# Four small edits to a hybrid decoder trunk: the lambda rows' tile and place, the step of the sums of squares, a PSUM bank passed over, the order of three ScalarE instructions

## The chip, the cores and the metric

The kernel runs on one core of one Trainium2 chip. The metric is the device time of one launch in microseconds (us), the median over runs; lower is better.

## What is computed

A decoder trunk of two layers over 512 tokens of width 1024, all in float32. Each sub-layer is normalised first (RMSNorm) and added back. Cut to what matters here:

```python
# layer 0: differential attention, 8 heads of 2 x 64, values 128 wide
qkv = rmsnorm(h, attn_norm) @ w_in
lam = exp(sum(lq1 * lk1)) - exp(sum(lq2 * lk2)) + lambda_init      # four rows of 64
logits = q @ k.T * 64**-0.5 + bias        # T5 relative bias, causal; two maps per head
p = softmax(logits);  attn = p[:, 0] - lam * p[:, 1]
h = h + (rmsnorm(attn @ v, subln) * (1 - lambda_init)) @ w_out
h = h + square(relu(rmsnorm(h) @ w1)) @ w2                        # MLP, 4096 wide
# layer 1: mLSTM, 4 heads, q and k 128 wide, v 256 wide
proj = rmsnorm(h, mlstm_norm) @ w_in      # q,k | v | output gate | i and f gates (8 columns)
q, k = silu(causal_conv(proj_qk, width=4))
num, den = gated causal sums over keys of (q.k) * v and of (q.k)
ht = num / max(|den|, exp(-m));  out = sigmoid(o_pre) * rmsnorm(ht) 
h = h + out @ w_out
h = h + square(relu(rmsnorm(h) @ w1)) @ w2
return rmsnorm(h, final_norm)
```

## The kernel before

Activations lie transposed, features on the 128 partitions and 512 tokens along the free axis: `h` is eight tiles of 128x512. Every operand of a large product is split in a high and a low part (`split`: ScalarE writes the high part with a Copy, VectorE the rest), and a product is three matmuls: high x high, high x low, low x high (`mm3`, lines 406 to 408; 438 to 440 for value products, 928 to 930 in the MLP's second half).

**Weights** come in units of 128x1024 through rings of three buffers `raw`, `whi`, `wlo` (`unit`, `issue`). SP loads `raw`; ScalarE and VectorE split it. For the query and key columns of the mLSTM it is done otherwise (lines 351 to 353): ScalarE writes `whi` and the negated high part into `wlo`, and GpSimd (POOL) issues a DMA that adds the weights onto `wlo`. The product of the unit waits for that transfer.

**Order.** TensorE's (PE) order is the program's. Each product step of three (or six) matmuls ends with `tick()`, which runs what was put off with `after(n, fn)`, n steps ahead. The order on the other engines is made by a scheduler from its own estimates; within an engine instructions run in order.

**Opening.** `arrive(k)` makes the operand of feature tile k (`operand`: `x_xh` on ScalarE, `x_xl` on VectorE, line 519). `square_in` adds up squares in `acc`, on POOL from k = 1. `attention` runs `group_mm` (32 steps: queries and keys of heads 0 and 1, four banks), then `values_of(0, "sc")` (16 steps: the values of heads 0 and 1, into two of the three "sc" banks), then per head two `ntile_mm` of 8 steps. At step `T_RS` `token_scale` splits `acc`, multiplies by ones (lines 541 and 542), and makes `rs`, the token scale, in `rsqrt2` (lines 555 to 559, three ScalarE and two VectorE steps in `chains`) and line 567. `head` evicts queries and keys times `rs` (lines 709, 710) and splits them into halves (716 to 720; the queries' low half on POOL, 719). `constants`, put off to step 31, loads the four lambda rows into a `tmp` tile (line 672), multiplies and sums them (673, 680) and writes `coef`. `bias_rows` makes the bias rows, which go to DRAM and come back skewed (lines 642 to 653), per head. The first score products (736, 737) use the same "sc" banks as the values: the second one waits for the last eviction of `values_of(0)` (`evict_v`, lines 587 and 588).

**mLSTM start.** Three banks are called "mm", three "ac", two "sc". `vpair_mm(x, 264)` makes the first values and the gate columns in one "mm" and three "ac" banks (`psv`), which `gates` evicts 12 steps later, behind `rs`. Then eight `ntile_mm` follow, queries and keys by turns, each evicted by `evict_qk`: times `rs` into the one `conv` tile (line 1054), three taps on VectorE (1058), a Sigmoid on ScalarE, a product (1063 or 1065), and a split whose low half is POOL's. `bank("mm")` takes the banks in turn, so the third `ntile_mm` comes to the "mm" bank that holds values. `gate_rows` (from 1095: transposes, scans 1097 and 1103, rows `gs`) and `gate_cols` (1115) run between the tiles at steps 28 and 62.

**mLSTM heads.** `squares` evicts the numerator (`of`), squares it, and reads the bank `pf` with an Exp into `dd` (line 1188); the head's next score product waits for that bank.

Of the kernel before, what the change touches and what calls it, by code (L numbers as in the profile page):

```python
# [19 lines left out]
P = 128  # L20
T = 512
D = 1024
KT = D // P
# [15 lines left out]

T_RS, T_RSC, T_CONST, T_BIAS, T_ROWS = 24, 39, 31, 4, 14
T_ONE, T_TWO = 3, 12


# [140 lines left out]
def trunk(ctx: ExitStack, tc, xT, wgt, wgt2, cols, rows, rel, consts, outT):  # L186
# [11 lines left out]
    def nm(s):  # L198
        return f"{s}_{next(names)}"
# [22 lines left out]
    def tmp(n=T):  # L222
        return sp.tile([P, T], F32, tag="tmp", name=nm("tmp"))
# [5 lines left out]
    def asf(t):  # L229
        return t.bitcast(F32)  # L230
# [19 lines left out]
    def act(out, x, func, **kw):  # L250
        name = {AF.Exp: LNSET, AF.Ln: LNSET, AF.Sigmoid: SGSET}.get(func)
        if name:
            tables(name)
        ins = nc.scalar.activation(out, x, func, **kw)  # L254
        if name:
            behind(ins, loaded["load"])
            loaded["uses"].append(ins)
# [7 lines left out]
    def after(n, fn):  # L265
        heapq.heappush(queue, (clock[0] + n, next(names), fn))
# [232 lines left out]
    def row_of(c, n):  # L499
        return bass.AP(tensor=rows.tensor, offset=rows.offset + c, ap=[[0, P], [1, n]])  # L500

    def col(c):
        return colt[:, c : c + 1]
# [8 lines left out]
    lneps = const_col(math.log(EPS), "lneps")  # L512


    def operand(k, g0, acc):
        hi = xp.tile([P, T], F32R, tag="x", name=nm("xh"))
        lo = xp.tile([P, T], F32R, tag="x", name=nm("xl"))
        act(hi, h[k], AF.Copy, scale=col(g0 + k))
        vec.scalar_tensor_tensor(lo, h[k], col(g0 + k), asf(hi), op0=ALU.mult, op1=ALU.subtract)  # L519
        if acc is not None:  # L520
            square_in(k, acc)
        return lambda: (hi, lo)
# [95 lines left out]
    def attention(x, acc):  # L618
        with ExitStack() as st:
# [47 lines left out]
            klow = [[ap_.tile([P, T], F32R, name=f"kl{b}{m}") for m in range(2)] for b in range(2)]  # L667
            STEPS = (((3, 0),), ((2, 0),), ((1, 0), (0, 256)))

            def constants():  # L670
                rowt, prod = tmp(), tmp()
                nc.gpsimd.dma_start(rowt[:, :256], row_of(0, 256))
                vec.tensor_tensor(
                    prod[:, 0:128].rearrange("p (a d) -> p a d", a=2),
                    rowt[:, 0:256].rearrange("p (a b d) -> p a b d", a=2, b=2)[:, :, 0],
                    rowt[:, 0:256].rearrange("p (a b d) -> p a b d", a=2, b=2)[:, :, 1],
                    op=ALU.mult,
                )
                dots = tmp()
                vec.tensor_reduce(  # L680
                    dots[:, 0:2], prod[:, 0:128].rearrange("p (a d) -> p a d", a=2),
                    axis=mybir.AxisListType.X, op=ALU.add,
                )
                act(dots[:, 0:2], dots[:, 0:2], AF.Exp)
                vec.memset(coef, 1.0)
                vec.tensor_tensor(dots[:, 2:3], dots[:, 1:2], dots[:, 0:1], op=ALU.subtract)
                for c in (1, 3):
                    vec.tensor_scalar(coef[:, c : c + 1], dots[:, 2:3], -LAM0, None, op0=ALU.add)
                vec.tensor_scalar(subw, col(C_SUB), -0.5 * (1.0 - LAM0), None, op0=ALU.mult)
                for pair in klow:  # L690
                    for m in range(2):
                        o = slice(64 - 64 * m, 128 - 64 * m)
                        vec.tensor_scalar(pair[m][o], ones_f[o].to_broadcast([64, T]), 0.0, None, op0=ALU.mult)
                filled(pth[:, 1408:1536], 0.0)
                filled(ptl[:, 1408:1536], 0.0)
# [119 lines left out]
            def values_of(j, tag="mm"):  # L815

                def done(ps, b):
                    until(lambda: summed[0] >= 2 * j)
                    if b == 0:
                        vt.clear()  # L820
                        new.append(value_tiles(vp))
                    evict_v(ps, b, rsc[0], *new[0])

                new = []
                vpair_mm(x, 256, done, tag)
                vt[j] = new[0]
# [4 lines left out]
            after(T_RSC, lambda: rsc.append(token_cols(rs)))  # L831
            ps = group_mm(x)
            head(0, ps[0], ps[1], T_ONE)
            head(1, ps[2], ps[3], T_ONE + T_TWO)
            values_of(0, "sc")
            for hd in range(2, AH):
                psq, psk = ntile_mm(x), ntile_mm(x)
                head(hd, psq, psk)
                if hd % 2 == 1 and hd < AH - 1:
                    values_of(hd // 2)  # L840
# [168 lines left out]
    def mlstm(x, acc):  # L1009
        with ExitStack() as st:  # L1010
# [60 lines left out]
            def gates(psv):  # L1071

                rsc.append(token_cols(rs))
                for tb in range(NB):
                    vec.scalar_tensor_tensor(gi[:, tb], psv[tb][:, 256:260], rsc[0][:, tb : tb + 1],
                                             gate_bias[:, 0:4], op0=ALU.mult, op1=ALU.add)
                    vec.scalar_tensor_tensor(gf[:, tb], psv[tb][:, 260:264], rsc[0][:, tb : tb + 1],
                                             gate_bias[:, 4:8], op0=ALU.mult, op1=ALU.add)
                vec.tensor_scalar(ab, gf, -1.0, None, op0=ALU.mult)
                vec.tensor_tensor(ab, ab, gf, op=ALU.min)  # L1080
                act(ab, ab, AF.Exp)
                act(ab, ab, AF.Ln, bias=1.0)
                vec.tensor_scalar(gf, gf, 0.0, None, op0=ALU.min)
                vec.tensor_tensor(gf, gf, ab, op=ALU.subtract)
                vt[0] = value_tiles(vp)
                for j in range(2):
                    evict_v(psv, j, rsc[0], *vt[0])
# [31 lines left out]
            def head(hd):  # L1119
# [56 lines left out]
                def squares():  # L1176
                    num0, num1, den = acc3
                    summed[0] += 1
                    pf = bank("sc")
                    mm(pf, sel[:, hs], gs[:, 1280:1792], start=True, stop=True)  # L1180
                    dd, d2, s0, s1 = scale_tile("rs2"), tmp(), chain("sq"), tmp()
                    of = [sg.tile([P, T], F32, tag="of", name=nm("of"), bufs=2) for _ in range(2)]
                    act(of[0], num0, AF.Copy)
                    vec.tensor_copy(of[1], num1)
                    act(s0, of[0], AF.Square)
                    act(s1, of[1], AF.Square)
                    pool.tensor_tensor(s0, s0, s1, op=ALU.add)
                    act(dd, pf, AF.Exp, scale=-2.0, bias=lneps)
                    act(d2, den, AF.Square, scale=math.sqrt(EPS))
                    vec.tensor_tensor(dd, dd, d2, op=ALU.max)  # L1190
                    after(D_MLS[hd][2], lambda: normed(s0, dd, of))
# [48 lines left out]

            after(T_MRS, lambda: token_scale(acc, rs))
            psv = vpair_mm(x, 264)
            after(T_GATES, lambda: gates(psv))
            after(T_GROWS, gate_rows)
            after(T_GCOLS, gate_cols)
# [174 lines left out]
```

## Time and profile before

| | |
|---|---|
| median of 3 runs | 1175.04 us (1174.48 to 1175.22) |
| the profiled execution | 1175.75 us, span 1174.0 us |
| mean granted clock of TensorE | 0.992 |
| TensorE busy | 1143.0 us, 97% |
| VectorE (DVE) busy | 899.4 us, 77% |
| ScalarE (ACT) busy | 616.4 us, 53% |
| GpSimd (POOL) busy | 191.7 us, 16% |
| read from HBM | 112.30 MB |

The profile is one execution. A timeline row gives start, length, engine, line of the kernel, operation, output tile<-inputs, shape and, in brackets, the idle time ahead of it and what ended that. A matmul's recorded length overlaps the next one's; what counts is the distance from start to start. An idle time costs something only on the engine that holds up the end, which is for the most part TensorE.

### The profile page before, as it was taken

How to read it: one execution, taken by the hardware profiler on the slowest of the kernel's cores; microseconds unless marked ns; L12 is line 12 of the kernel's file. 1: busy time of each engine (PE TensorE's matmuls, PEld its weight loads, DVE VectorE, ACT ScalarE, POOL GpSimd, SP SyncE). 2: the span in 40 equal slices, each digit the busy share in tenths (PEclk: the TensorE clock that was granted, in tenths of full speed). 3: DMA queues.
4: the chain of work that ended last, by engine and by line, in shares of the span. 5: the costliest groups of instructions: out<-in, count | busy, mean ns of one | idle time of the engine just before them, and what ended most of it. 6: DMA issues, size and time to landing. Idle time of an engine off the chain costs nothing.

```text
span 1174.0 us, 17210 instructions
## 1 busy us (share of the span) xinstructions
PE 1143.0 (97%) x6718; PEld 1006.1 (86%) x6718; DVE 899.4 (77%) x1371; ACT 616.4 (53%) x926; POOL 191.7 (16%) x186
## 2 busy tenths in 40 slices
PE   8899999999999999999999999999999999999996
PEld 5778888888898998998997789888889889889895
DVE  7789888587977866967968867766698687687786
ACT  6567777564534434434557547665454353353453
POOL 5432332040000000000132212233000000000001
PEclk9899999999999999999999999999999999999998
DMA  6622222143164264362366221123325525526412
GB/s 203 203 64 75 78 73 78 65 123 123 61 168 138 64 180 134 84 169 90 92 155 147 68 90 55 54 80 104 122 82 135 161 73 139 173 66 153 135 37 72
DMA packets 37745, 128.12 MB, mean 109 GB/s; under 512 B 4479, under 2 KB 6546, under 8 KB 37664
## 3 DMA queue, kind: packets, MB, share of 16 engines
q1 hardware_dynamic: 30288, 103.38, 27.6%
q0 software_dynamic: 6256, 22.07, 9.8%
q10 hardware_dynamic: 1120, 1.57, 0.4%
q8 instruction: 53, 0.87, 0.3%
q14 instruction: 28, 0.23, 0.1%
HBM read 112.30 MB, written 4.74 MB: 100 GB/s over the span
## 4 chain that ended last, share of the span: by engine, by line
PE 81%; DVE 11%; ACT 4%; DMA 2%; issue 2%; POOL 0%; DVEq 0%; SPq 0%; ACTq 0%; POOLq 0%
PE bank L407 15%; PE bank L408 15%; PE bank L406 15%; PE bank L929 8%; PE bank L930 8%; PE bank L928 8%; DVE tmp_tmp L1058 2%; PE bank L439 1%; PE bank L438 1%; PE bank L440 1%; DVE wlo L534 1%; DMA raw<-wgt 1%; ACT whi L254 1%; PE bank L736 1%; DVE kl L720 1%
## 5 line engine op out<-in xcount | busy, mean ns | idle before, releaser
L406 PE MATMUL bank<-x_xh,whi 128*128 128x512 f32 x640 | 254.1, 397 | 4.0 <-DVE vl_v L588 2.5
L407 PE MATMUL bank<-x_xl,whi 128*128 128x512 f32 x640 | 254.9, 398 | 0.6 <-DVE x_xl L519 0.6
L408 PE MATMUL bank<-x_xh,wlo 128*128 128x512 f32 x640 | 255.4, 399 | 0.0
L254 ACT ACTIVATE whi<-raw 128x1024 fp32r<-128x1024 f32 (+2 forms) x128 | 133.4, 1042 | 115.6 <-PE bank L929 43.3
L534 DVE TENSOR_TENSOR wlo<-raw,whi 128x1024 fp32r<-128x1024 f32 (+2 forms) x120 | 152.9, 1274 | 30.2 <-ACT whi L254 29.5
L929 PE MATMUL bank<-ul,whi 128*128 128x256 f32 x544 | 153.3, 282 | 0.1
L928 PE MATMUL bank<-uh,whi 128*128 128x256 f32 x544 | 153.3, 282 | 0.0
L930 PE MATMUL bank<-uh,wlo 128*128 128x256 f32 x544 | 153.2, 282 | 0.0
L406 PEld LDWEIGHTS bank<-x_xh,whi 128*128 128x128 f32 x640 | 122.8, 192 | 32.2 <-DVE vl_v L588 3.0
L407 PEld LDWEIGHTS bank<-x_xl,whi 128*128 128x128 f32 x640 | 121.4, 190 | 28.1 <-DVE x_xl L519 1.3
L408 PEld LDWEIGHTS bank<-x_xh,wlo 128*128 128x128 f32 x640 | 121.1, 189 | 27.1 <-DVE wlo L534 0.2
L949 POOL DMA_DIRECT2D h<-work x24 | 20.8, 865 | 511.6 <-DVE work L946 392.5
L929 PEld LDWEIGHTS bank<-ul,whi 128*128 128x128 f32 x544 | 102.7, 189 | 0.5 <-DVE ul L534 0.3
L928 PEld LDWEIGHTS bank<-uh,whi 128*128 128x128 f32 x544 | 103.0, 189 | 0.1
L930 PEld LDWEIGHTS bank<-uh,wlo 128*128 128x128 f32 x544 | 102.8, 189 | 0.0
L254 ACT ACTIVATE uh<-chains 128x1792 fp32r<-128x1792 f32 (+1 forms) x38 | 56.9, 1497 | 57.6 <-DVE chains L889 57.4
L534 DVE TENSOR_TENSOR ul<-chains,uh 128x1792 fp32r<-128x1792 f32 (+1 forms) x38 | 67.3, 1771 | 23.8 <-ACT uh L254 23.3
L882 DVE SCALAR_TENSOR_TENSOR tmp_tmp<-bank,rs_rs 128x512 f32<-128x512 f32 x64 | 44.0, 688 | 44.7 <-PE bank L408 44.5
L530 POOL TENSOR_TENSOR acc_acc<-acc_acc,tmp_tmp 128x512 f32<-128x512 f32 x31 | 50.9, 1642 | 157.5 <-ACT tmp_tmp L254 152.5
L254 ACT ACTIVATE whi<-wsums 128x1024 fp32r<-128x1024 f32 x46 | 48.7, 1059 | 48.2 <-PE bank L929 30.2
L439 PE MATMUL bank<-wlo,x_xh 128*128 128x256 f32 (+1 forms) x256 | 72.2, 282 | 1.7 <-DVE wlo L534 1.7
L438 PE MATMUL bank<-whi,x_xh 128*128 128x256 f32 (+1 forms) x256 | 72.6, 284 | 0.0
(332 smaller groups left out, 2683.2 us busy)
## 6 DMA issues: line engine op xcount, KB each, us to landing
raw<-wgt SPq DMA_DIRECT2D x156, 512.0 KB, 3.8
rawx<-wgt SPq DMA_DIRECT2D x32, 512.0 KB, 4.1
h<-work POOLq DMA_DIRECT2D x24, 512.0 KB, 5.8
wlo<-wgt POOLq DMA_DIRECT2D x8, 512.0 KB, 7.3
skew<-frd POOLq DMA_DIRECT2D x8, 320.0 KB, 6.8
bias_bias<-skew POOLq DMA_DIRECT2D x8, 256.0 KB, 3.1
outT<-h SPq DMA_DIRECT2D x6, 256.0 KB, 2.5
raw<-wgt SPq DMA_DIRECT2D x2, 528.0 KB, 3.6
```

What stands on the lines that cost most here:

```text
L254: ins = nc.scalar.activation(out, x, func, **kw)
L406: mm(ps, whi, x[0], start=first, stop=False)
L407: mm(ps, whi, x[1], start=False, stop=False)
L408: mm(ps, wlo, x[0], start=False, stop=last)
L438: mm(ps, xh, hi[:, c], start=k == 0, stop=False)
L439: mm(ps, xh, lo[:, c], start=False, stop=False)
L530: (eng or pool).tensor_tensor(acc, acc, s, op=ALU.add)
L534: (eng or vec).tensor_tensor(lo, src, asf(hi), op=ALU.subtract)
L882: vec.scalar_tensor_tensor(m, p, 0.0, rs, op0=ALU.max, op1=ALU.mult)
L928: mm(out[name], hi[:, n], uh[:, t], start=first, stop=False, skip_group_check=late)
L929: mm(out[name], hi[:, n], ul[:, t], start=False, stop=False, skip_group_check=late)
L930: mm(out[name], lo[:, n], uh[:, t], start=False, stop=k == 3, skip_group_check=late)
```

## The change

- `constants`: the rows get a tile of their own, `rowt`, in place of three `tmp` tiles; their load is put off by 3 steps from the start of `attention`, not to step 31; the first product is bound behind the last operand's low part (`lows[KT - 1]`), as an order on VectorE alone.
- `T_RS` goes from 24 to 27: the sums of squares are multiplied three steps later.
- `head(1, ...)` is called behind `values_of(0, "sc")`, 16 steps later, with its wait lowered by 16.
- in `squares` the factor `dd` is written first.
- in `mlstm` the "mm" bank that holds values is taken out of the turn for 20 steps.

```diff
-T_RS, T_RSC, T_CONST, T_BIAS, T_ROWS = 24, 39, 31, 4, 14
+T_RS, T_RSC, T_CONST, T_BIAS, T_ROWS = 27, 39, 31, 4, 14
...
+    lows = {}
+
     def operand(k, g0, acc):
...
-        vec.scalar_tensor_tensor(lo, h[k], col(g0 + k), asf(hi), op0=ALU.mult, op1=ALU.subtract)
+        lows[k] = vec.scalar_tensor_tensor(lo, h[k], col(g0 + k), asf(hi), op0=ALU.mult, op1=ALU.subtract)
...
+            rowt = ap_.tile([P, 388], F32, name="rowt")
+            after(3, lambda: nc.gpsimd.dma_start(rowt[:, :256], row_of(0, 256)))
+
             def constants():
-                rowt, prod = tmp(), tmp()
-                nc.gpsimd.dma_start(rowt[:, :256], row_of(0, 256))
-                vec.tensor_tensor(
+                prod, dots = rowt[:, 256:384], rowt[:, 384:388]
+                first_dots = vec.tensor_tensor(
...
-                dots = tmp()
+                behind(first_dots, lows[KT - 1])
...
             head(0, ps[0], ps[1], T_ONE)
-            head(1, ps[2], ps[3], T_ONE + T_TWO)
             values_of(0, "sc")
+            head(1, ps[2], ps[3], T_ONE + T_TWO - 16)
...
+                    act(dd, pf, AF.Exp, scale=-2.0, bias=lneps)
                     act(of[0], num0, AF.Copy)
                     vec.tensor_copy(of[1], num1)
                     act(s0, of[0], AF.Square)
                     act(s1, of[1], AF.Square)
                     pool.tensor_tensor(s0, s0, s1, op=ALU.add)
-                    act(dd, pf, AF.Exp, scale=-2.0, bias=lneps)
...
             psv = vpair_mm(x, 264)
+
+            kept = turn["mm"].pop()
+            after(20, lambda: turn["mm"].append(kept))
             after(T_GATES, lambda: gates(psv))
```

What the scheduler makes of it shows in the instructions' order on each engine. Lines of the changed kernel are up to 7 higher. The first place is VectorE at the end of the opening group, from the lambda product to the weight split behind the evictions. Before (`wlo_92`: the low part of a weight unit; `tmp`: the lambda tiles first, the evicted queries and keys of heads 0 and 1 last):

```order
L673 TENSOR_TENSOR tmp_tmp_233<-tmp_tmp_204 128x128
L680 TENSOR_REDUCE tmp_tmp_255<-tmp_tmp_233 128x2
L558 TENSOR_TENSOR chains<-chains 128x512
L686 TENSOR_TENSOR tmp_tmp_255<-tmp_tmp_255 128x1
L559 SCALAR_TENSOR_TENSOR chains<-chains 128x512
L688 TENSOR_SCALAR coef<-tmp_tmp_255 128x1 x2
L567 TENSOR_SCALAR rs_rs_183<-chains 128x512
L709 SCALAR_TENSOR_TENSOR tmp_tmp_195<-bank_77,rs_rs_183 128x512
L710 TENSOR_TENSOR tmp_tmp_204<-bank_78,rs_rs_183 128x512
L709 SCALAR_TENSOR_TENSOR tmp_tmp_233<-bank_79,rs_rs_183 128x512
L710 TENSOR_TENSOR tmp_tmp_255<-bank_80,rs_rs_183 128x512
L534 TENSOR_TENSOR wlo_92<-raw_86,whi_89 128x1024
```

Now, from the low part of the sums (`sl_sl`) on; the lambda product and its reduction stand just above these rows:

```order
L536 TENSOR_TENSOR sl_sl_347<-acc_acc_128,sh_sh_346 128x512
L690 TENSOR_TENSOR rowt<-rowt 128x1
L692 TENSOR_SCALAR coef<-rowt 128x1 x2
L536 TENSOR_TENSOR wlo_94<-raw_88,whi_91 128x1024
L567 TENSOR_SCALAR chains<-bank_83 128x512
L560 TENSOR_TENSOR chains<-chains 128x512
L561 SCALAR_TENSOR_TENSOR chains<-chains 128x512
L569 TENSOR_SCALAR rs_rs_184<-chains 128x512
L536 TENSOR_TENSOR wlo_92<-raw_86,whi_89 128x1024
L713 SCALAR_TENSOR_TENSOR tmp_tmp_205<-bank_77,rs_rs_184 128x512
L714 TENSOR_TENSOR tmp_tmp_235<-bank_78,rs_rs_184 128x512
L713 SCALAR_TENSOR_TENSOR tmp_tmp_257<-bank_79,rs_rs_184 128x512
```

The lambda steps have left the token scale's chain, one weight split (`wlo_94`) stands ahead of the eviction of the sums, and another (`wlo_92`) ahead of the evictions of head 0. On ScalarE the exponential of lambda now stands ahead of the high half `whi_91`.

The second place is TensorE at the end of the second and the start of the third of the eight query and key tiles of the mLSTM. Before (`bank_81` holds the first values, `bank_77` and `bank_79` are the other two "mm" banks):

```order
L406 MATMUL bank_77<-x_xh_314,whi_90 128x512
L407 MATMUL bank_77<-x_xl_315,whi_90 128x512
L408 MATMUL bank_77<-x_xh_314,wlo_93 128x512
L406 MATMUL bank_81<-x_xh_129,whi_91 128x512 [waits DVE_49]
L407 MATMUL bank_81<-x_xl_130,whi_91 128x512
L408 MATMUL bank_81<-x_xh_129,wlo_94 128x512 [waits DMASW7_49]
```

Now:

```order
L406 MATMUL bank_77<-x_xh_316,whi_90 128x512
L407 MATMUL bank_77<-x_xl_317,whi_90 128x512
L408 MATMUL bank_77<-x_xh_316,wlo_93 128x512
L406 MATMUL bank_79<-x_xh_129,whi_91 128x512 [waits DVE_49,Activation_49]
L407 MATMUL bank_79<-x_xl_130,whi_91 128x512
L408 MATMUL bank_79<-x_xh_129,wlo_94 128x512 [waits DMASW7_49]
```

The third tile has moved from the values' bank to the bank of the first tile; the fourth then takes `bank_77`. The third place is ScalarE in `squares` of the first mLSTM head (`rs_0_rs` is the factor `dd`, `bank_84` is `pf`). Before:

```order
L254 ACTIVATE of_of_5858<-bank_80 128x512
L254 ACTIVATE sh_sh_5684<-e_e_5674 128x512
L254 ACTIVATE chains<-of_of_5858 128x512
L254 ACTIVATE tmp_tmp_195<-of_of_5859 128x512
L254 ACTIVATE rs_0_rs_336_2325<-bank_84,lneps 128x512
L254 ACTIVATE tmp_tmp_255<-bank_83 128x512
```

Now:

```order
L254 ACTIVATE of_of_5859<-bank_80 128x512
L254 ACTIVATE sh_sh_5685<-e_e_5675 128x512
L254 ACTIVATE rs_0_rs_334_2326<-bank_84,lneps 128x512
L254 ACTIVATE chains<-of_of_5859 128x512
L254 ACTIVATE tmp_tmp_205<-of_of_5860 128x512
L254 ACTIVATE tmp_tmp_196<-bank_83 128x512
```

The factor has moved up by two instructions here and in the third head; in the second and fourth the order is as it was, one square ahead of it.

## The prediction

> **What bounds the kernel.** I read the page first, then what TensorE (PE) waits for, then the clock around the long waits, then the timelines there.
>
> ```profile
> PE 1143.0 (97%) x6718; PEld 1006.1 (86%) x6718; DVE 899.4 (77%) x1371; ACT 616.4 (53%) x926; POOL 191.7 (16%) x186
> PE 81%; DVE 11%; ACT 4%; DMA 2%; issue 2%; POOL 0%; DVEq 0%; SPq 0%; ACTq 0%; POOLq 0%
> ```
>
> PE is busy for 97% of the span and carries 81% of the chain that ended last. The change leaves its products alone, so only waits of PE (31 us in all) and slow matmuls after them can be won.
>
> ```profile
> PE bank L406 <- DVE vl_v L588: 3.3, 2, 2.5
> PE bank L736 <- DVE vl_v L588: 3.1, 2, 2.4
> PE bank L542 <- DVE sl_sl L534: 1.9, 1, 1.9
> PE bank L439 <- DVE wlo L534: 1.7, 1, 1.7
> PE bank L1145 <- ACT rs_rs L254: 1.2, 1, 1.2
> PE bank L1145 <- DVE e_e L1148: 1.0, 1, 1.0
> ```
>
> Columns: total us, times, longest. The first row's 2.5 us and the 1.7 and 1.0 us lie at the start of the mLSTM; the second and third rows in the first 55 us; the fifth in an mLSTM head.
>
> ```profile
> 12.00:15.00 3.00, 2.50 (x10) 1.48 (x9) 1.37 (x2) 2.88 (x6) 0.52 (x1) 1.00 1.05 395
> 53.90:58.00 4.10, 4.09 (x16) 3.82 (x17) 3.55 (x13) 1.54 (x5) 0.00 (x0) 0.61 0.72 232
> 619.80:624.00 4.20, 4.20 (x12) 3.29 (x13) 3.79 (x8) 4.17 (x7) 0.34 (x1) 0.59 0.01 2
> ```
>
> Busy times per stretch, then granted clock, DMA share, GB/s. After the waits of 2.4 and 2.5 us the clock was 0.61 and 0.59 for 4 us. Twelve matmuls took 4.20 us; at the usual 0.233 us from start to start (the rows at 37.21 and 37.45 below) they are 2.80, so such a wait costs 1.4 us more behind itself.
>
> **Part 1: Lambda rows, sums of squares, head 1 (0 to 54 us).**
>
> ```profile
> 27.51 1.21 DVE L534 TENSOR_TENSOR wlo<-raw,whi 128x1024 fp32r<-128x1024 f32 x1
> 29.45 0.67 DVE L534 TENSOR_TENSOR sl_sl<-acc_acc,sh_sh 128x512 fp32r<-128x512 f32 x1
> 31.73 1.96 ACT L254 ACTIVATE chains<-chains 128x512 f32<-128x512 f32 x3 [3.08 <-DVE chains L565]
> 36.81 0.29 DVE L673 TENSOR_TENSOR tmp_tmp<-tmp_tmp 128x128 f32<-128x128 f32 x1 [3.99 <-DMA tmp_tmp<-rows]
> 37.21 0.40 PE L408 MATMUL bank<-x_xh,wlo 128*128 128x512 f32 x1
> 37.45 0.28 PE L438 MATMUL bank<-whi,x_xh 128*128 128x256 f32 x1
> 38.79 0.42 DVE L567 TENSOR_SCALAR rs_rs<-chains 128x512 f32<-128x512 f32 x1
> 39.32 0.69 DVE L709 SCALAR_TENSOR_TENSOR tmp_tmp<-bank,rs_rs 128x512 f32<-128x512 f32 x1
> 40.04 0.63 ACT L254 ACTIVATE q_q<-tmp_tmp 64x512 fp32r<-64x512 f32 x1 [1.42 <-DVE tmp_tmp L709]
> 40.30 0.57 POOL L653 DMA_DIRECT2D bias_bias<-skew  x1 [1.40 <-DMA skew<-frd]
> 40.93 1.29 POOL L719 TENSOR_TENSOR q_q<-tmp_tmp,q_q 64x512 fp32r<-64x512 f32 x1
> 41.72 1.58 DVE L534 TENSOR_TENSOR wlo<-raw,whi 128x1024 fp32r<-128x1024 f32 x1
> 43.23 4.19 DVE L720 TENSOR_TENSOR kl<-tmp_tmp,kh_kh 64x512 fp32r<-64x512 f32 x3
> 53.91 0.77 PE L736 MATMUL bank<-kh_kh,q_q 128*128 128x512 f32 x1 [2.40 <-DVE vl_v L588]
> tmp_tmp<-rows POOLq DMA_DIRECT2D x1, 128.0 KB, 3.5
> ```
>
> (Start, length, engine, line, tiles; in brackets the wait ahead.) Before, DVE stands 3.99 us for the lambda rows in the middle of the token scale, with rs and the evictions of heads 0 and 1 queued behind; PE then waits at 53.91 for the last value eviction of that chain. Now the rows are loaded third on POOL's queue, long before 27 us, and that wait goes.
>
> The new DVE chain: the product (0.2) stands at 27.51, the weight split moves to 27.7, reduce and two copies (1.0) follow, and the low half of the sums starts at 29.9 and ends at 30.57, 0.45 late. PE runs nine matmuls (2.1 us) that it held back, from 27.1 to 29.2, does the high half, waits 1.0 us for the low half (before 1.9) and starts it at 30.6. Matmuls after waits of 1.0 and 1.7 us (675.46 and 660.40, part 2) are 0.4 us long, not 0.6 as under the slow clock, so no clock loss is taken here; if there is one, it is at most 1.4 us of PE, of which DVE's chain hides all but some 0.5. Fifteen matmuls (3.5 us) end the group at 34.35, before at 37.45. ACT's exponential of lambda now stands ahead of a weight's high half, which starts at 29.4; its low half on DVE therefore runs from 30.8 to 32.0, ahead of the eviction of the sums (0.69), so that one is 1 us later than before. ACT's three steps (1.96) end at 34.65, two DVE steps (1.3) and rs start at 36.0; a weight split (1.2) that stood behind the evictions is now ahead, and the first eviction L709 starts at 37.55 against 39.32: 1.8 us earlier, no more. The split is no longer in the chain behind: 4 evictions (2.4), then key splits, value evictions and two weight splits. ACT starts its first copy 0.72 behind L709, at 38.3 (before 40.04), does twelve copies of 0.61 to 0.63 and two value halves of 0.4 up to 46.5, then weight, value, weight, value (1.0 and 0.4 each), the last behind DVE's eviction of the one before. DVE's four key splits, slowed by POOL (4.19 us for three, where an unhindered half tile takes 0.69), end at 48.1, a weight split at 49.3, three short evictions and the first score step near 50.9. PE would have been at that product at 53.91 less its two waits of 3.1, that is 13.35 us behind 37.45: now at 47.7. It waits 3.2 us and pays the slow clock as before. 53.91 less 50.9 is 3.0 us.
>
> Moved past: POOL's queue has the rows ahead of three small loads for the bias rows, which PE makes only in the group's third unit; the copies for the bias come 0.45 us later, so the first bias load at 40.75, needed by 49.8; the second bias load is now ahead of the four q subtractions, which start at about 42.0, not 40.93, and have until 47: hidden. Against it: the 128 KB now fall into the opening burst, where the transfers run at 395 GB/s, share 1.05, and PE follows the weights closely: 0.33 us. **Sum of part 1: -2.6 us**, bounds -1.4 (only L709's 1.77, less 0.33) and -3.3. Head 1's scores keep their step (three fewer ahead, sixteen back): nothing.
>
> **Part 2: the bank passed over (604 to 676 us).**
>
> ```profile
> 612.27 0.69 DVE L1054 TENSOR_TENSOR conv<-bank,rs_rs 128x512 f32<-128x512 f32 x1
> 617.88 0.68 DVE L1054 TENSOR_TENSOR conv<-bank,rs_rs 128x512 f32<-128x512 f32 x1
> 619.72 0.51 PE L406 MATMUL bank<-x_xh,whi 128*128 128x512 f32 x1 [2.54 <-DVE vl_v L588]
> 623.43 1.04 ACT L254 ACTIVATE wlo<-raw 128x1024 fp32r<-128x1024 f32 x1
> 624.76 0.87 POOL L353 DMA_DIRECT2D wlo<-wgt  x1 [4.63 <-ACT wlo L254]
> wlo<-wgt POOLq DMA_DIRECT2D x1, 512.0 KB, 7.8
> wlo<-wgt POOLq DMA_DIRECT2D x2, 512.0 KB, 6.3
> 627.16 0.69 DVE L1054 TENSOR_TENSOR conv<-bank,rs_rs 128x512 f32<-128x512 f32 x1 [1.45 <-PE bank L408]
> 629.74 0.60 PE L1095 MATMUL bank<-ident,gi 128*4 128x128 f32 x4
> 633.84 1.21 DVE L1097 TENSOR_TENSOR_SCAN mr<-lf,ig 4x512 f32<-4x512 f32 x1
> 643.51 0.63 ACT L254 ACTIVATE tmp_tmp<-tmp_tmp 128x512 f32<-128x512 f32 x1 [1.85 <-DVE tmp_tmp L1058]
> 655.36 0.22 PE L1115 MATMUL bank<-ident,ig 4*128 4x4 f32 x1 [0.61 <-DVE ig L1105]
> 660.40 0.39 PE L439 MATMUL bank<-wlo,x_xh 128*128 128x256 f32 x1 [1.70 <-DVE wlo L534]
> 675.46 0.44 PE L1145 MATMUL bank<-qk_qkh,qk_qkh 128*128 128x384 f32 x1 [0.99 <-DVE e_e L1148]
> ```
>
> Query/key tile 2 (counted from 0) stood in the bank of the first values and waited 2.54 us. Now it takes tile 0's bank, read out at 612.27, and tile 3 that of tile 1, read out at 617.88: PE goes on at 617.0. Tile 2 (24 x 0.233 = 5.6 us) ends at 622.6, tile 3 with its transposes (6.4) at 629.0. What is late next is tile 4's low weights: ACT writes them at 623.43 and POOL issues their adding transfer at 624.76, both in the order of before; it landed 7.8 us on, at 632.6 (second transfer row, of this one alone). PE had its first need at 633.9; now at 629.5. It waits 3.1 us and pays 1.4 of clock: with 22 more matmuls (5.1) tile 4 ends at 639.1, before at 633.86 plus 5.1, 639.0. So the wait that is removed comes back, one and a half tiles later.
>
> The gain is what DVE gets. It evicts tile 2 at 623.6 instead of 627.16, does a product at 625.0 behind ACT's sigmoid, and five steps of some 0.67 us to 629.2, where the scan of 633.84 starts; a product (0.7) that stood ahead of the scan now follows, so it is 3.9 us ahead. ACT takes some back: two weight copies (1.04 each) wait for tile 4's end at 639.1 and stand ahead of a sigmoid, which goes from 643.51 to 641.2: 2.3 us ahead, and DVE keeps 2.2 of it. Tiles 5 to 7 then run unhindered, and the waits of 0.61, 1.70 and 0.99 us, all on DVE's chain, shrink by 2.2 together: **-2.2 us**, bounds 0 and -3.3, the sum of the three.
>
> **Part 3: the head's factor on ScalarE.** In heads 0 and 2 it moves up two instructions (1.2 us); in 1 and 3 the order is what it was, and head 1 holds the 1.2 us wait on it. No PE wait is listed in the other two: 0, bounds +-0.6.
>
> **Sum.** -2.6 - 2.2 = -4.8 us from the profiled 1175.75 (span 1174.0): 1170.95. The median of the runs shown, 1175.04, is 0.71 under that execution: 1170.2.
>
> **Rivals.**
> - The adding transfers of tiles 4 to 7 queue one behind another: landings 632.6, 640.4, 648.2, 656.0, 7.8 apart. PE then waits at 5, 6 (2.2 us, with slow clock) and 7, is 4.8 us late at the value products and takes the 2.7 of 1.70 and 0.99 back: +2.1, with part 1 -0.5, 1174.5; where they overlap in part, some 1173.3. Against: two of them issued within 5 us of each other landed in 6.3. It decides for slower once they lie 8.8 us apart: three times 1.0 us more gives +2.5, 1177.5.
> - The opening gives nothing: PE comes earlier but the value evictions end where they did, since POOL's subtractions, one us later, slow DVE's key splits and value evictions longer. For it: 4.19 us for three splits. Against: the weight split is out of that stretch. Only -2.2: 1172.8.
> - The clock holds through both 3.1 us waits: 1.4 more in part 1, 1.1 in part 2, so 1167.7. Against: 0.61 and 0.59 after shorter waits.
>   [...]
>
> **Chances.** My sum (1169.0 to 1171.6) 0.52; opening gives nothing 0.16; queued transfers 0.16, of which 0.04 over 1177.4; clock holds 0.10; else 0.06. The range leaves out the ends: 1168.0 to 1173.3. Against 0.2% (2.35 us, what a measurement here can tell): faster 0.78 (mine, the clock, half of the opening's, some rest), same 0.18, slower 0.04.
>
> **What would show it.** DVE without the 4 us wait before the lambda product, first L709 (now L713) near 37.5; the scores at 53.91 near 51; no PE wait at 617, one of about 3 us near 632 on the low weights, clock near 0.6 behind it; the wait at 660 gone; the 1.2 us wait in head 1 still there. I am wrong if the low weights land sooner or later than PE needs, or the value evictions do not move.

## Result, and the profile after

The changed kernel takes 1169.89 us (median of 7 runs, 1168.51 to 1172.65); the kernel before took 1175.41 beside it. The ratio is 0.9947, with a 95% interval of 0.9932 to 0.9962: 5.5 us less. In a second set on another chip the ratio was 0.9933 (0.9919 to 0.9946). My number was 1170.2.

The profiled execution of the changed kernel is its slowest, 1172.65 us (span 1170.8): only 3.1 us under the profiled one of before. Why single executions differ that much becomes half of the story. First the busy times and the chain of work that ended last, of the changed kernel:

```profile
PE 1141.7 (98%) x6718; PEld 1005.7 (86%) x6718; DVE 898.6 (77%) x1371; ACT 616.4 (53%) x926; POOL 190.5 (16%) x186
PE 81%; DVE 9%; ACT 5%; DMA 2%; issue 2%; POOL 0%; DVEq 0%; SPq 0%; ACTq 0%; POOLq 0%
```

VectorE's share of the chain fell from 11% to 9%. What PE waits for (total us, times, longest):

```profile
PE bank L408 <- DMA wlo<-wgt: 3.5, 1, 3.5
PE bank L740 <- DVE vl_v L590: 3.1, 1, 3.1
...
PE bank L1149 <- ACT rs_rs L254: 1.2, 1, 1.2
PE bank L406 <- ACT x_xh L254: 1.1, 1, 1.1
PE bank L544 <- DVE sl_sl L536: 1.0, 1, 1.0
...
PE bank L1149 <- DVE e_e L1152: 0.4, 1, 0.4
```

The bank wait at tile 2, the wait of 1.7 us for a low half and that of 0.6 for the gate rows are gone; the first row is the new wait that the prediction named. The timeline of the opening, and then of the mLSTM's start:

```profile
28.63 0.28 DVE L677 TENSOR_TENSOR rowt<-rowt 128x128 f32<-128x128 f32 x1
31.68 0.50 PE L544 MATMUL bank<-sl_sl,ones_d 128*128 128x512 f32 x1 [1.00 <-DVE sl_sl L536]
38.65 0.68 DVE L713 SCALAR_TENSOR_TENSOR tmp_tmp<-bank,rs_rs 128x512 f32<-128x512 f32 x1
51.06 0.48 DVE L590 SCALAR_TENSOR_TENSOR vl_v<-bank,rscol_rscol,vh_v 128x256 fp32r<-128x256 f32 x1
51.69 0.47 PE L740 MATMUL bank<-kh_kh,q_q 128*128 128x512 f32 x1 [3.13 <-DVE vl_v L590]
```

```profile
622.97 0.87 POOL L353 DMA_DIRECT2D wlo<-wgt  x1 [4.61 <-ACT wlo L254]
627.56 1.21 DVE L1101 TENSOR_TENSOR_SCAN mr<-lf,ig 4x512 f32<-4x512 f32 x1
631.26 0.80 PE L408 MATMUL bank<-x_xh,wlo 128*128 128x512 f32 x1 [3.47 <-DMA wlo<-wgt]
639.45 0.69 DVE L1058 TENSOR_TENSOR conv<-bank,rs_rs 128x512 f32<-128x512 f32 x1 [1.66 <-PE bank L408]
641.13 0.62 ACT L254 ACTIVATE tmp_tmp<-tmp_tmp 128x512 f32<-128x512 f32 x1
672.31 0.44 PE L1149 MATMUL bank<-qk_qkh,qk_qkh 128*128 128x384 f32 x1 [0.44 <-DVE e_e L1152]
wlo<-wgt POOLq DMA_DIRECT2D x1, 512.0 KB, 8.3
```

The lambda product has no wait ahead of it (before: 3.99 us). The score product of 53.91 stands at 51.69. The adding transfer lands 8.3 us after its issue, at 631.27, where PE's wait ends. VectorE's eviction of the same tile then waits 1.66 us for PE, at 639.45.

**Two marks** cut the program into three pieces: VectorE's eviction of the mLSTM's first sums, and the product in mLSTM head 1 that waits for the factor. Before, then after:

```profile
606.29 0.69 DVE L565 TENSOR_SCALAR chains<-bank 128x512 f32<-128x512 f32 x1 [6.07 <-PE bank L542]
720.09 0.50 PE L1145 MATMUL bank<-qk_qkh,qk_qkh 128*128 128x512 f32 x1 [1.23 <-ACT rs_rs L254]
```

```profile
604.48 0.69 DVE L567 TENSOR_SCALAR chains<-bank 128x512 f32<-128x512 f32 x1 [6.05 <-PE bank L544]
716.95 0.50 PE L1149 MATMUL bank<-qk_qkh,qk_qkh 128*128 128x512 f32 x1 [1.23 <-ACT rs_rs L254]
```

The same marks in the profiled executions of most kernels that follow, in us (the medians are of several chips; ratios are given with each experiment); "steps" are stretches of half clock of 3.41 us each (1.7 us of clock), counted from the granted clock microsecond by microsecond, in the opening (to the first score products) and at the mLSTM's start:

| kernel | to mark 1 | mark 1 to 2 | rest | steps | median of runs, lowest to highest |
|---|---|---|---|---|---|
| before | 606.29 | 113.80 | 453.91 | 2, 1 | 1176.31 (1173.97 to 1179.23, 23 runs) |
| factor alone | 606.23 | 114.02 | 453.85 | 2, 1 | 1175.95 (1173.79 to 1177.67) |
| bank alone | 610.42 | 112.20 | 453.88 | 3, 2 | 1174.26 (1171.28 to 1178.25) |
| part 1 alone | 603.10 | 114.01 | 453.99 | 1, 1 | 1172.90 (1172.63 to 1173.27) |
| rows alone | 604.49 | 113.95 | 453.86 | 2, 1 | 1174.64 (1173.32 to 1175.63) |
| changed | 604.48 | 112.47 | 453.85 | 1, 2 | 1169.89 (1168.51 to 1172.65) |
| changed, again | 603.74 | 112.20 | 453.86 | 1, 2 | 1169.51 (1168.36 to 1171.55) |
| rows late | 602.91 | 110.89 | 453.90 | 0, 1 | 1169.49 (1167.51 to 1169.58) |
| tile 4 on POOL | 604.49 | 110.00 | 453.91 | 2, 0 | 1169.77 (1168.88 to 1170.27) |
| idle products | 602.41 | 110.87 | 453.92 | 0, 0 | 1169.19 (1168.90 to 1169.52) |
| tile 4 on POOL, idle products | 602.40 | 109.75 | 453.85 | 0, 0 | 1168.24 (1167.72 to 1168.52) |

The rest is the same to 0.14 us, so all that happened lies in the first two columns.

### The profile page after: what moved, and what is told of

It reads as the page before. It is cut to its first block, busy times and chain, and to the rows that moved or that the text cites. A ratio compares the mean times of both kernels' runs of the same rounds, so it can differ in the third digit from the quotient of the medians.

```text
span 1170.8 us, 17209 instructions
## 1 busy us (share of the span) xinstructions
PE 1141.7 (98%) x6718; PEld 1005.7 (86%) x6718; DVE 898.6 (77%) x1371; ACT 616.4 (53%) x926; POOL 190.5 (16%) x186
## 4 chain that ended last, share of the span: by engine, by line
PE 81%; DVE 9%; ACT 5%; DMA 2%; issue 2%; POOL 0%; DVEq 0%; SPq 0%; ACTq 0%; POOLq 0%
PE bank L408 15%; PE bank L407 15%; PE bank L406 15%; PE bank L933 8%; PE bank L934 8%; PE bank L932 8%; PE bank L439 1%; PE bank L438 1%; PE bank L440 1%; DMA raw<-wgt 1%; DVE wlo L536 1%; DVE tmp_tmp L1062 1%; ACT chains L254 1%; ACT whi L254 1%; DMA wlo<-wgt 1%
```

## Experiments

**Each part alone**, in the kernel before. Part 1 alone is the changed kernel without the lines of the other two parts.

```diff
+            kept = turn["mm"].pop()                       # bank alone
+            after(20, lambda: turn["mm"].append(kept))
```

```diff
+                    act(dd, pf, AF.Exp, scale=-2.0, bias=lneps)   # factor alone
                     act(of[0], num0, AF.Copy)
...
-                    act(dd, pf, AF.Exp, scale=-2.0, bias=lneps)
```

> The first part alone, in the kernel before: the lambda rows in their own tile, their product behind the operands, the sums of squares three steps later, head 1's move; no bank passed over, the factor where it was. My recorded working gives -2.6 us against the kernel before (bounds -1.4 and -3.3). The rival that the opening gives nothing gives 0 to +0.4 (PE is earlier but the value evictions end where they did). A third reading, from the profiled execution of the whole change, where the start of the program cost 1.1 us instead of my 0.33 and the score product came 2.2 us earlier: -2.2. By each theory the profile has no 4 us wait of DVE before the lambda product; by mine the score product at 53.91 starts near 51.

> The bank passed over, alone, in the kernel before. My recorded working gives -2.2 us (bounds 0 and -3.3). Read from the profiled execution of the whole change, where the wait at tile 4 was 3.47 us and the slow clock behind it held for 6 us and not 4: -1.3. The rival, that wait and slow clock simply move from tile 2 to tile 4, gives 0. In each the wait of 2.5 us at tile 2 is gone and one of 3 to 3.5 us for tile 4's low weights stands in its place; the wait of 1.7 us near 660 tells the theories apart: gone by the first two, still there by the third.

> A head's factor first on ScalarE, alone, in the kernel before. My recorded working gives 0 +- 0.6 us, since the order changes only in heads 0 and 2 and the 1.2 us wait on the factor is in head 1. The rival, that the heads gain where no wait of PE is listed (the factor releases the stage behind it), gives -0.6 or more. If the three parts add up, this one is what is left of -5.5 us after the other two.

Ratios to the kernel before on the same chip: part 1 0.9969 (0.9957 to 0.9981), -3.6 us; the bank 0.9981 (0.9967 to 0.9994), -2.2; the factor 0.9996 (0.9986 to 1.0006), -0.5, not to be told from nothing, and its piece between the marks did not shrink (114.02 against 113.80). The sum is -6.3, about what the whole change gave. Two things stand out. Part 1 gave 1 us more than I had for it (my 2.6 is still inside its interval, 2.2 to 5.1), and its five runs lie within 0.6 us, all at a clock of 0.994, where the kernel before spreads over 5 in 23 runs. And the bank alone has the new wait:

```profile
PE bank L736 <- DVE vl_v L588: 5.6, 2, 3.7
PE bank L408 <- DMA wlo<-wgt: 3.2, 1, 3.2
```

The first of these rows belongs to the opening, which this edit leaves alone; in the profiled execution of before it was 3.1 us. It leads to the lambda wait on VectorE, here in the kernel with the bank alone:

```profile
39.79 0.29 DVE L673 TENSOR_TENSOR tmp_tmp<-tmp_tmp 128x128 f32<-128x128 f32 x1 [7.63 <-DMA tmp_tmp<-rows]
tmp_tmp<-rows POOLq DMA_DIRECT2D x1, 128.0 KB, 6.1
```

The wait that I priced from one execution at 3.99 us (landing 3.5 us after issue) was 7.63 in this one (landing 6.1).

**Rows alone**: part 1 with `T_RS` at 24 and head 1 in its old place.

> Of the first part only the lambda rows in a tile of their own, loaded early, and their product behind the operands; the sums of squares at their old step, head 1 in its old place, no bank passed over, the factor where it was. By my recorded working the 4 us wait of DVE is what costs, and the later sums only make room on PE: rows alone give most of part 1, -1.8 to -2.6 us against the kernel before, and the wait of 1.9 us for the low half of the sums stays, with its slow clock (which the whole first part, -3.4 us, does without). Rival: the product now stands ahead of the sums' low half on DVE and makes it 0.5 us later, so that PE waits 2.4 us there with a slow clock that holds up the whole group: 0 to -0.8.

```profile
30.89 0.50 PE L544 MATMUL bank<-sl_sl,ones_d 128*128 128x512 f32 x1 [2.07 <-DVE sl_sl L536]
36.47 0.69 DVE L713 SCALAR_TENSOR_TENSOR tmp_tmp<-bank,rs_rs 128x512 f32<-128x512 f32 x1 [0.45 <-PE bank L408]
40.56 5.35 DVE L724 TENSOR_TENSOR kl<-tmp_tmp,kh_kh 64x512 fp32r<-64x512 f32 x3
46.01 1.60 DVE L724 TENSOR_TENSOR kl<-tmp_tmp,kh_kh 64x512 fp32r<-64x512 f32 x1
52.16 0.48 DVE L590 SCALAR_TENSOR_TENSOR vl_v<-bank,rscol_rscol,vh_v 128x256 fp32r<-128x256 f32 x1
52.79 0.47 PE L740 MATMUL bank<-kh_kh,q_q 128*128 128x512 f32 x1 [1.35 <-DVE vl_v L590]
```

The first and last eviction and the score product of part 1 alone:

```profile
38.00 0.68 DVE L713 SCALAR_TENSOR_TENSOR tmp_tmp<-bank,rs_rs 128x512 f32<-128x512 f32 x1
50.42 0.48 DVE L590 SCALAR_TENSOR_TENSOR vl_v<-bank,rscol_rscol,vh_v 128x256 fp32r<-128x256 f32 x1
51.05 0.77 PE L740 MATMUL bank<-kh_kh,q_q 128*128 128x512 f32 x1 [3.21 <-DVE vl_v L590]
```

Ratio 0.9983 (0.9975 to 0.9992), -2.0 us: inside what I gave the rows. Between the two medians, the later sums with head 1's move are worth the other 1.6, which I had at nothing. PE's wait at the sums stays without them (2.07 us), and a step of half clock follows at 32 us. But that is not the main delay of the scores. PE's lateness holds up VectorE's first eviction by 0.45 us and ScalarE twice by 0.3 to 0.4 us near 49 and 50 us, yet the first eviction, at 36.47, is 1.5 us earlier than in part 1 alone. What is longer is VectorE's stretch from there to the start of the last value eviction: 15.7 us against 12.4. Here the four key splits (`kl`) run ahead of all value evictions and take 6.95 us beside POOL's subtractions; in part 1 alone they stand between the value evictions and take 3.86. A weight split of 1.2 us that stands ahead of the first eviction there lies inside the stretch here. So the score product comes at 52.79 and not at 51.05. Which of the two edits sets this order was not run apart. The other step in this execution's opening, at 14 us, stands behind a wait of 1.84 us for an operand.

**The changed kernel again**, with the two that follow on the same chip.

> The changed kernel again, beside the other three. Theory of the slow clock in steps: in the profiled executions so far the clock after a wait of PE was at half for stretches that cost 1.7, 3.4 or 5.1 us of clock (one, two or three times 3.4 us of half clock), and which it is changes from one execution to the next. Then the times scatter by steps of about 1.5 us, with a granted clock that falls 0.0015 with each step, over 3 to 5 us in all, median 5 to 6 us under the kernel before. Rival: the scatter of the changed kernel comes from the opening (transfers), and the granted clock is the same in its fast and slow executions.

Its runs and their granted clocks: 1168.36 and 1168.38 (0.996); 1169.29 and 1169.74 (0.994); 1171.51 and 1171.55 (0.993 and 0.992). That is the first theory's picture: groups, and the clock falls with each. In the first seven runs the order is less clean (1168.51 at 0.994, 1169.22 at 0.996). The mean clock is a rough measure: it also counts half clock behind PE's last product, where nothing waits for PE (in the profiled execution of the first set PE's last product ends at 1161.56, and the clock is 0.50 from 1163.0 to the end at 1170.8).

**Idle products** in the changed kernel, so that PE does not stand still at its two long waits:

```diff
+    def keep_warm(x, n):
+        for _ in range(n):
+            mm(turn["ac"][-1], ones_d, x[0]()[0], start=True, stop=True)
...
+                        if hd == 0 and s == 0 and m == 1:
+                            keep_warm(x, 12)
...
+            if warm and k == 0:      # tile 4 alone: warm = 12
+                mm(ps, hi[:, c], x[0]()[0], start=True, stop=False)
+                mm(ps, hi[:, c], x[0]()[1], start=False, stop=False)
+                keep_warm(x, warm)
+                mm(ps, lo[:, c], x[0]()[0], start=False, stop=False)
```

> The changed kernel with twelve idle products of 512 columns (2.8 us at full clock, into a bank that nobody reads) at each of PE's two long waits: ahead of head 0's second score product (wait 3.1 us) and ahead of tile 4's first product with the low weights (wait 3.1 to 3.5 us). They add nothing to the work on the path as long as the waits last. Theory of the slow clock in steps: PE no longer idles there, so no half clock follows (stretches near 52 and 630 gone), and the executions no longer differ by steps: median 1.2 to 2.5 us under the changed kernel, all executions within 1.5 us, the fastest where the changed kernel's fastest is. Rival: DVE's chain binds behind both waits and PE's slow products cost nothing: median within 0.5 us of the changed kernel, with its scatter.

The stretches from 50 to 60 and from 628 to 640 us (busy times, granted clock, DMA share, GB/s), in the changed kernel and then with idle products:

```profile
50.00:60.00 10.00, 8.05 (x32) 6.67 (x33) 7.69 (x29) 4.78 (x17) 1.81 (x3) 0.83 0.37 107
628.00:640.00 12.00, 8.74 (x26) 6.91 (x27) 10.28 (x16) 4.81 (x8) 2.16 (x2) 0.72 0.77 185
```

```profile
50.00:60.00 10.00, 9.43 (x45) 7.46 (x44) 7.51 (x30) 5.17 (x18) 1.81 (x3) 1.00 0.41 129
628.00:640.00 12.00, 12.00 (x54) 9.68 (x53) 11.52 (x19) 6.55 (x10) 4.11 (x4) 1.00 0.63 142
```

The clock stays at 1.00 and the five runs lie within 0.6 us: the scatter was the clock. But the ratio to before, 0.9940 (0.9926 to 0.9953), cannot be told from the changed kernel's, and the median, 1169.19, is 0.3 to 0.7 under its two medians, against the 1.2 to 2.5 that I expected. So in a typical execution much of the half clock was hidden; it shows in the longest ones. The profiled executions give its price. From the lambda product to mark 1, kernels with the whole first part took 574.7 to 574.8 us with no step at the scores, 575.2 to 575.9 with one, 576.4 with two. From mark 1 to 2 it was 110.9 with no step at tile 4 (here) and with one (rows late, below), 112.2 to 112.5 with two. Here another wait has come in, of 1.53 us for tile 7's low weights, so VectorE is not the only thing behind tile 4. (The scheduler also set a few VectorE steps of tiles 5 to 7 in another order, so the second column is not an exact comparison.)

**Tile 4's low half on POOL**: this takes the wait away, and leaves the bank passed over.

```diff
+                if u == FIRST_QK + 4:
+                    split(raw[:, c], hi[:, c], lo[:, c], nc.gpsimd)
-                if PLAN[u][0] == "m_in" and PLAN[u][1][0][1] < D:
+                elif PLAN[u][0] == "m_in" and PLAN[u][1][0][1] < D:
```

> The changed kernel, but the low half of the weights of query/key tile 4 (counted from 0) is made by POOL's subtraction from the high half, instead of ACT's second copy and an adding transfer. Theory: what the passed-over bank gives back is the late landing of exactly this transfer (3.47 us of wait and some 3 us of slow clock). POOL needs about 2.6 to 3.3 us for 1024 columns (1.29 to 1.63 us for 512), so the low half is there near 625 and PE needs it at 627.8: the wait goes. Tile 5's transfer, issued at 627.0 and landing 7 to 8.6 us on, is next: PE needs it near 633.4 and waits 0.6 to 2.2 us. DVE's eviction of tile 4 no longer waits 1.66 us for PE, nor the product behind it 1.64 us for ACT, so I expect 1 to 3 us under the changed kernel. Rival: DVE is bound there anyway (POOL's subtraction slows it, its scans fill 640 to 660), and the time stays within 0.5 us of the changed kernel.

The wait of 3.5 us and its clock are gone, but PE now waits

```profile
PE bank L442 <- DVE wlo L539: 1.1, 1, 1.1
...
PE bank L1152 <- DVE e_e L1155: 1.0, 1, 1.0
...
PE bank L1122 <- DVE ig L1112: 0.8, 1, 0.8
```

all on VectorE. Between the marks it takes 110.00 us where the changed kernel took 112.47 and 112.20 with two steps of half clock and 110.89 (rows late, below) with one. The ratio to before, 0.9940 (0.9928 to 0.9952), cannot be told from the changed kernel's: the rival was right about the median. In this kernel VectorE is the bound behind tile 4.

**Three more units' low halves on POOL**, to relieve VectorE there (`u - FIRST_QK in (4, 8, 9, 10)` in the diff above).

> The kernel with tile 4's low weights made by POOL, and also the low halves of three later units (the two of the next values and the first output gate's) by POOL's subtraction instead of DVE's. In the profile of the kernel with tile 4 alone PE waited 1.1 us for such a low half, 0.8 us for DVE's gate rows and 1.0 us for DVE's score step, so there DVE binds. Theory: three splits of 1.2 us leave DVE, the three waits shrink by 2 to 2.9 us, so 2 to 3 us under the kernel with tile 4 alone. Rival: POOL needs some 3 us for each, slows DVE by the same amount while both run (as in the opening, where DVE's operand steps took 1.7 us beside POOL's sums and 0.75 alone), and nothing is left: within 0.5 us of it.

It is some 4.7 us slower than the changed kernel, which neither theory had: 1174.26 us, 0.9974 (0.9964 to 0.9984). Between the marks it takes 114.28 us, against 110.00 with tile 4 alone. Rows of VectorE and POOL, and PE's longest wait:

```profile
641.95 3.48 POOL L539 TENSOR_TENSOR wlo<-raw,whi 128x1024 fp32r<-128x1024 f32 x1
642.46 0.71 DVE L1065 SCALAR_TENSOR_TENSOR tmp_tmp<-conv,colt,tmp_tmp 128x512 f32<-128x512 f32 x1
643.11 2.47 DVE L1112 TENSOR_TENSOR ig<-ig,pr 4x128 f32<-4x128 f32 x1
650.09 3.16 POOL L539 TENSOR_TENSOR wlo<-raw,whi 128x1024 fp32r<-128x1024 f32 x1
650.98 2.42 DVE L1112 TENSOR_TENSOR ig<-ig,pr 4x128 f32<-4x128 f32 x1
PE bank L1122 <- DVE ig L1112: 5.0, 1, 5.0
```

A VectorE subtraction of 0.27 us (in the kernel with tile 4 alone) lasted until POOL's ended, twice: 4.4 us, in the one engine that had none to give, and as much as the stretch between the marks grew.

**Rows late**: the lambda rows loaded near 17 us, out of the opening burst.

```diff
-            after(3, lambda: nc.gpsimd.dma_start(rowt[:, :256], row_of(0, 256)))
+                behind(vec.memset(rowt[:, 0:1], 0.0), lows[2])
+                nc.gpsimd.dma_start(rowt[:, :256], row_of(0, 256))
```

> The changed kernel with the lambda rows loaded near 17 us instead of near 3 us (behind the third operand's low half and the first sum of squares), so out of the opening burst; their product still finds them at 28.6. My recorded price of the rows in the burst is 0.33 us; the profiled executions so far have PE's last product before 22 us that waits for an operand at 19.9, 19.9, 20.3 without the rows in the burst and 20.7, 20.9, 21.4 with them, which makes 0.9. Theory: 0.3 to 0.9 us under the changed kernel. Rival: DVE's chain and the value evictions set the end of this part, and PE's earlier start only makes its wait near 51 longer: 0.

1169.49 against 1169.51 us, ratio to before 0.9928 (0.9916 to 0.9940): no gain that can be told. PE's product that waits for an operand near 21 stood at 20.87, inside the spread of the kernels with the rows in the burst. What pushes it from 20 to 21 in those kernels stays open. This execution had no half clock in the opening though PE waited the same 3.1 us there:

```profile
50.00:60.00 10.00, 8.61 (x41) 7.12 (x42) 7.71 (x29) 5.17 (x18) 1.81 (x3) 1.00 0.39 115
```

Tile 4's eviction in the same execution, and the sigmoid behind it:

```profile
636.28 0.69 DVE L1062 TENSOR_TENSOR conv<-bank,rs_rs 128x512 f32<-128x512 f32 x1
637.96 0.62 ACT L254 ACTIVATE tmp_tmp<-tmp_tmp 128x512 f32<-128x512 f32 x1
```

Behind the wait at tile 4 (3.1 us) there was one step of half clock here, and the eviction does not wait for PE; with two steps it waited 1.66 us in the profiled execution of the changed kernel and 1.34 in the second. The stretch between the marks is shorter by nearly these amounts, 1.6 and 1.3 us.

**Head 0's scores five steps later** (`T_ONE, T_TWO = 8, 7`).

> The changed kernel with head 0's score products five steps later, so that PE has fifteen products of the next tile (3.5 us) to do where it waits 3.1 us for the last value eviction; head 1's scores keep their step. Theory: the wait at 51.7 is a matter of PE's order only (the second score product needs a bank of the values, the tile behind it does not), so the wait and the slow clock behind it go: 3 to 4.5 us under the changed kernel. Rival: the attention's first head is bound by DVE and ACT (softmax, splits) and PE waits the same 3 us a little later, for a probability or an eviction: within 0.6 us of the changed kernel.

```profile
51.70 0.47 PE L740 MATMUL bank<-kh_kh,q_q 128*128 128x512 f32 x1 [0.22 <-DVE vl_v L590]
67.83 0.66 PE L740 MATMUL bank<-kh_kh,q_q 128*128 128x384 f32 x1 [2.94 <-DVE ptl L778]
96.68 0.77 PE L789 MATMUL bank<-pth,vh_v 128*128 128x512 f32 x1 [6.24 <-DVE sm_sm L755]
```

The wait at 51.7 went, and came back as 2.9 and 6.2 us behind VectorE's softmax of later heads: 1179.42 us, some 10 slower than the changed kernel. Mark 1 came at 613.15, 9.4 us later than in the changed kernel on the same chip, with two steps of half clock at each of the two waits. Both theories were wrong; why VectorE is late for the later heads was not followed further.

**Idle products in the kernel before**, 7, 9 and 9 at its three long waits.

> The kernel before with idle products at its three long waits: 7 ahead of the low half of the first sums of squares (wait 1.9 us), 9 ahead of head 0's second score product (2.4 us), 9 ahead of query/key tile 2 (2.5 us). Theory of the slow clock in steps: the three stretches of half clock near 30, 54 and 620 go, the executions lie within 1.5 us of each other, and the median is 1.5 to 3 us under the kernel before; the distance to the changed kernel with idle products, 4 to 5 us, is then what the change gives in waits alone, as my recorded sum has it (4.8 with the clock the same on both sides). Rival: most of what the change gave was clock: then this kernel is within 2 us of the changed kernel with idle products.

This one did not answer its question: 1184.15 us, 8 slower. The scheduler put the lambda product ahead of the eviction of the sums, and the nine idle products at tile 2 went into a bank of values that was not yet read out:

```profile
38.24 0.29 DVE L680 TENSOR_TENSOR tmp_tmp<-tmp_tmp 128x128 f32<-128x128 f32 x1 [7.15 <-DMA tmp_tmp<-rows]
PE bank L412 <- DVE vl_v L595: 4.3, 1, 4.3
```

So what before would take with its clock held was not measured. It shows again how much hangs on the lambda rows: here the wait was 7.15 us, and mark 1 came at 610.55.

**Tile 4 on POOL and idle products at the score product together.**

> The kernel with tile 4's low weights made by POOL, and twelve idle products ahead of head 0's second score product. Theory that the stages add up: from the profiled executions, the program up to the first statistics of the mLSTM ends at 602.4 us where idle products kept the clock in the opening (603 to 604.5 without them), the stretch from there to the factor's product in head 1 takes 110.0 us with tile 4 on POOL (110.9 with idle products at tile 4, 112.2 to 112.5 in the changed kernel, 113.8 before), and the rest takes 453.9 in every kernel so far: span 1166.3, time near 1168.0, 1.5 to 2 us under the changed kernel and some 8 under the kernel before, all executions within 1.5 us. Rival: the executions of the kernel with tile 4 on POOL were already undisturbed in the median and the opening's DVE chain binds: 1169 to 1170, no better than either.

1168.24 us, ratio to before 0.9927 (0.9913 to 0.9941), and the pieces add up: 602.40 and 109.75. Its median is the shortest here, 1.3 to 1.7 us under the changed kernel's two, with all runs within 0.8; by the ratios, each to the kernel before on its own chip, the two intervals overlap.

## Why the prediction was right, and where it was off

- **Lambda wait and opening, -2.6.** The mechanism held: no wait ahead of the lambda product, PE's score product between 51.0 and 51.9 (my sum gives 50.9 and 0.33 for the burst), its wait of 3.1 to 3.2 us still there. Against the profiled execution of before, part 1 alone had the score product 2.9 us earlier and mark 1 3.2 earlier. In the medians it gave 3.6 (2.2 to 5.1), so the size was rather too small, and one term was taken from too little: I had the lambda wait as 3.99 us; it was 3.99 to 7.63 in the four executions profiled with the rows in their old place, and the change removes all of it. How often it is long was not counted. I gave the later sums and head 1's move nothing of their own; the kernel with rows alone shows that they go with VectorE's order of key splits and value evictions and are worth some 1.6 us. I had four key splits at the length that they have before, 5.8 us; they took 3.9 in part 1 alone and 4.8 in the profiled execution of the changed kernel. That no half clock follows a wait of 1.0 us was right in every profiled execution that had one.
- **First eviction at 37.55.** It came at 38.65 in the profiled execution, 37.6 to 38.7 in the others with the whole part: late by the start of the program (the lambda product stands at 27.6 to 28.7, said: 27.5).
- **128 KB in the burst, 0.33.** Taking them out gained nothing that the runs can tell.
- **Bank, -2.2.** Alone -2.2 (0.7 to 3.9). The wait returned at tile 4's low weights with 3.1 to 3.5 us (said 3.1), and the transfer took 8.3 (said 7.8). The clock behind it was the mis-sized term: I had 1.4 us, as at tile 2; it was two steps, 3.4 us of clock, in three of the executions profiled with that wait (the two of the changed kernel and the bank alone), and one with rows late, so the piece between the marks shrank by 1.3 to 1.6 and by 2.9. In the kernel with head 0's scores later the wait was 2.5 us, with one step. That the median came out at my -2.2 is in part luck: it lies between these cases. VectorE's scan came 4.5 us earlier (6.3 less the 1.8 of the opening; said 3.9), and the waits of 1.70 and 0.61 are gone, as forecast. The sigmoid's 641.13 only looks like my 641.2, which was without the opening's gain: counted from mark 1 it came 0.6 us ahead, not 2.3, and 2.2 ahead with one step, in rows late. That VectorE binds behind tile 4 once the transfer is out of the way is shown by the kernel with tile 4 on POOL.
- **Factor, 0.** Measured -0.5, interval -1.6 to +0.7; the 1.2 us wait in head 1 is untouched.
- **Rivals.** Queued transfers: no wait for those of tiles 5 to 7 in the changed kernel (1.53 us for tile 7's with idle products). Opening gives nothing: refuted by part 1 alone. Clock holds: not in the two profiled executions of the changed kernel; of the six executions with the whole first part and the 3.1 to 3.2 us wait at the scores, it held in one.
- **The sum.** -4.8 against -5.5 in the medians of the first set and -7.5 in those of the second, where the kernel before took 1177.04 us. That 1170.2 lies 0.3 us from the first median, and 0.7 from the second, is partly luck: the gain was larger than my sum, and the kernel before stood higher than the 1175.04 that I started from.

## What to carry to other kernels

A wait priced from one profiled execution is one draw. Where the runs of a kernel scatter by several us, profile more than one, and look at landing times and at the clock behind each wait. Taking away a wait of varying length can gain more than its size in the best execution. Before a PE wait is removed, ask whether another engine is bound right behind it: here three of four attempts on PE's remaining waits ended at VectorE, and the fourth, the idle products, made the runs steady but moved the median by less than the runs can tell.

## What was not expected of the hardware

- **Half clock came in steps of 3.41 us, and their number differed between executions.** The profiled stretches cost 1.7, 3.4 or 5.1 us of clock; in the profiled execution of the changed kernel the granted clock was 0.50 for 3.41 us from 53.7 on and for 6.83 us from 630.5 on. After a wait of 3.1 to 3.2 us at the score product there were none, one or two; after 3.1 to 3.5 at tile 4 one or two; after 1.9 to 2.1 at the sums one in three executions, none in a fourth; after 1.8 to 2.3 for an operand near 14 us one in each of three executions (rows alone, three more units on POOL, head 0's scores later); after 1.0 at the sums, none. What sets the number was not shown. Half clock also followed waits of 1.8 to 2.6 us, which are shorter than one step.
- **A VectorE step beside POOL's subtraction lasted until that had ended**: 2.47 and 2.42 us for a step of 0.27. POOL's own were longer too, 3.48 and 3.16 us against 2.40 for tile 4's in the same execution. Not every step beside them was longer: the tap row ahead of the first such step, begun 0.5 us after POOL's, kept its 0.71 us. It is not special to these units: in the changed kernel a scan of 4x256 beside POOL's q and k split lasted 1.77 us; in the kernel before it began 0.47 us after that split had ended and lasted 0.67.
- **A 128 KB load landed 3.5 to 6.1 us after its issue** in the same place of the same code, with the skew transfers of the same queue right behind it in the long case (issued 0.6 us later, against 1.5 in the short one; two executions in between, 3.8 and 5.3 us, had 1.4 and 0.6).
